# Four heads on 32 partitions each: moving Q and K in 4 KB runs in a cross-covariance attention kernel

## The chip, the cores and the metric

The kernel runs on one core of one Trainium2 chip. Times are microseconds of the device for one whole execution. A profile's span goes from the first to the last instruction on the core and is some 2 us shorter than the time of the same run (138.7 against 140.83 us in the kernel before). The engines are PE (matrix multiply, with PEld for its weight loads), DVE (vector), ACT (scalar), POOL (GpSimd) and SP, which here only issues DMA.

On one core a run is marked slow when it is more than 1.5% above the fastest of the same kernel; comparisons use the fast runs.

## The reference, cut to what matters

```python
# Q, K, V: (8, 12, 512, 64) float32
Q_norm = Q / (norm of Q over the 512 rows + 1e-10)
K_norm = K / (norm of K over the 512 rows + 1e-10)
attn = einsum('bhnd,bhne->bhde', Q_norm, K_norm)      # 64 x 64 for each head
attn = softmax(attn, axis=-1)
return einsum('bhnd,bhde->bhne', V, attn)
```

There are 96 heads. Q, K, V and the output are 12.58 MB each, 50.3 MB in all, and the arithmetic is small, so a kernel that hides its compute is limited by the transfers (in the kernel before they are 76% of the chain that ended last).

## The kernel before

A unit is 4 heads, and 24 units go through a software pipeline. The norms and the products are had from one matrix: with x = [Q K] for one head (512 rows, 128 columns, bf16), the **gram** xᵀx holds QᵀQ, QᵀK and KᵀK. The diagonal gives the squared norms, and a corner gives the unscaled logits.

Q and K are loaded with 4 consecutive rows of one head on a partition, which is 4 x 64 x 4 B = 1 KB in one piece:

```python
Qf = Q.rearrange("b h (p t) d -> p (b h) t d", p=128)      # t = 4
Kf = K.rearrange("b h (p t) d -> p (b h) t d", p=128)
```

One gram is then 4 matmuls of 128 rows, 16 for a unit. The gram pool has two buffers, so two units' grams lie in different buffers of PSUM:

```python
ps_g = ctx.enter_context(tc.tile_pool(name="ps_g", bufs=2, space=bass.MemoryType.PSUM))
...
def grams(u):
    g = gram[u] = ps_g.tile([128, PU, 4, D], F32, name="gram")
    for h in range(HU):
        o = g[:, h // 2, 2 * (h % 2):2 * (h % 2) + 2, :]
        for t in range(T):
            x = qkb[u][:, h, t, :]
            nc.tensor.matmul(o, x, x, start=(t == 0), stop=(t == T - 1))
```

The order in which one pipeline step `s` issues its work is the order of each engine's queue:

```python
on(casts, s + CAST_AHEAD)   # DVE  f32 -> bf16 of Q and K
on(scale_k, s - 1)          # DVE  reads the gram, writes kqs
on(normalise, s - 2)        # DVE
on(grams, s)                # PE
on(norms, s)                # DVE  reads the gram; then POOL: power -1/2, gives rq
on(cast_v, s - 1)           # DVE
on(vtrans, s - 2)           # PE, then ACT
on(outs, s - 3)             # PE, then ACT
on(logits, s - 1)           # PE   kqs times an identity
on(doubled, s - 2)          # PE, then ACT
on(exps, s - 1)             # ACT
```

Of the kernel before, what the change touches and what calls it, by code (L numbers as in the profile page):

```python
# [8 lines left out]
F32 = mybir.dt.float32  # L9
BF16 = mybir.dt.bfloat16  # L10
AF = mybir.ActivationFunctionType
ALU = mybir.AluOpType

D = 64
T = 4
HU = 4
PU = HU // 2
RV = 16
NV = 512 // RV
HS = 128 // NV  # L20
SV = HU // HS
TP = RV // 2


@with_exitstack
def kernel(
# [9 lines left out]
    assert N == 128 * T and Q.shape[3] == D  # L36
    BH = B * H
    U = BH // HU



    Qf = Q.rearrange("b h (p t) d -> p (b h) t d", p=128)
    Kf = K.rearrange("b h (p t) d -> p (b h) t d", p=128)
    Vf = V.rearrange("b h n d -> (b h n d)").rearrange("(s p f) -> p s f", p=128, f=RV * D)
    Of = out.rearrange("b h n d -> (b h n d)").rearrange("(s p f) -> p s f", p=128, f=RV * D)
# [11 lines left out]
    ps_g = ctx.enter_context(tc.tile_pool(name="ps_g", bufs=2, space=bass.MemoryType.PSUM))  # L57
    ps_v = ctx.enter_context(tc.tile_pool(name="ps_v", bufs=2, space=bass.MemoryType.PSUM))
    ps_l = ctx.enter_context(tc.tile_pool(name="ps_l", bufs=1, space=bass.MemoryType.PSUM))
    ps_d = ctx.enter_context(tc.tile_pool(name="ps_d", bufs=1, space=bass.MemoryType.PSUM))  # L60
# [7 lines left out]
    qf, kf, vf, vb, qkb, gram, nsq, kqs, rq, lg, ex, at, ab, vt, so = ({} for _ in range(15))  # L68

    def load_qk(u):  # L70
        qf[u] = qp.tile([128, HU, T, D], F32, name="qf")
        kf[u] = qp.tile([128, HU, T, D], F32, name="kf")
        nc.sync.dma_start(out=qf[u], in_=Qf[:, u * HU:(u + 1) * HU])  # L73
        nc.sync.dma_start(out=kf[u], in_=Kf[:, u * HU:(u + 1) * HU])  # L74

    def load_v(u):
        vf[u] = vp.tile([128, SV, RV * D], F32, name="vf")
        nc.sync.dma_start(out=vf[u], in_=Vf[:, u * SV:(u + 1) * SV])  # L78

    def store(u):  # L80
        nc.sync.dma_start(out=Of[:, u * SV:(u + 1) * SV], in_=so[u])

    def casts(u):

        t_ = qkb[u] = qkp.tile([128, HU, T, 2 * D], BF16, name="qkb")
        nc.vector.tensor_copy(t_[:, 0::2, :, 0:D], qf[u][:, 0::2])  # L86
        nc.vector.tensor_copy(t_[:, 1::2, :, D:2 * D], qf[u][:, 1::2])
        nc.vector.tensor_copy(t_[:, 0::2, :, D:2 * D], kf[u][:, 0::2])  # L88
        nc.vector.tensor_copy(t_[:, 1::2, :, 0:D], kf[u][:, 1::2])  # L89

    def cast_v(u):
        w = vb[u] = vbp.tile([128, SV, TP, 2 * D], BF16, name="vb")
        nc.vector.tensor_copy(w.rearrange("p s t d -> p s (t d)"), vf[u])  # L93

    def grams(u):
        g = gram[u] = ps_g.tile([128, PU, 4, D], F32, name="gram")
        for h in range(HU):
            o = g[:, h // 2, 2 * (h % 2):2 * (h % 2) + 2, :]
            for t in range(T):
                x = qkb[u][:, h, t, :]  # L100
                nc.tensor.matmul(o, x, x, start=(t == 0), stop=(t == T - 1))  # L101

    def norms(u):

        n2 = nsq[u] = small.tile([128, 2, PU], F32, name="nsq")
        for p in range(PU):
            for c, (blk, m) in enumerate(((gram[u][:, p, 0::3, :], mask_q), (gram[u][:, p, 1:3, :], mask_k))):
                scr = small.tile([128, 2, D], F32, name="scr")
                nc.vector.tensor_tensor_reduce(  # L109
                    out=scr, in0=blk, in1=m, scale=1.0, scalar=1e-20,  # L110
                    op0=ALU.mult, op1=ALU.add, accum_out=n2[:, c, p:p + 1],
                )
        r = rq[u] = small.tile([128, 2, PU], F32, name="rq")
        nc.gpsimd.tensor_tensor(out=r, in0=n2, in1=mhalf, op=ALU.pow)  # L114

    def scale_k(u):

        kk = kqs[u] = small.tile([128, PU, 2, D], F32, name="kqs")
        for p in range(PU):
            nc.vector.scalar_tensor_tensor(  # L120
                out=kk[:, p], in0=gram[u][:, p, 0::3, :], scalar=rq[u][:, 1, p:p + 1], in1=off_diag,
                op0=ALU.mult, op1=ALU.mult,
            )

    def logits(u):
        l = lg[u] = ps_l.tile([128, PU, D], F32, name="lg")
        for p in range(PU):
            nc.tensor.matmul(l[:, p, :], kqs[u][:, p].rearrange("p a d -> p (a d)"), eye2)  # L128

    def exps(u):  # L130
        e = ex[u] = small.tile([128, PU, D], F32, name="ex")
        s = small.tile([128, PU], F32, name="esum")
        for p in range(PU):
            nc.scalar.activation(e[:, p, :], lg[u][:, p, :], AF.Exp, scale=rq[u][:, 0, p:p + 1], accum_out=s[:, p:p + 1])  # L134
        ex[u] = (e, s)

    def normalise(u):
        e, s = ex[u]
        ri = small.tile([128, PU], F32, name="rinv")
        nc.vector.reciprocal(ri, s)  # L140
        a = at[u] = small.tile([128, PU, D], BF16, name="at")
        for p in range(PU):
            nc.vector.tensor_scalar_mul(a[:, p, :], e[:, p, :], ri[:, p:p + 1])  # L143
# [120 lines left out]
```

## Time and profile before

| | before |
|---|---|
| time, median of 3 (range) | 141.01 us (140.42 to 141.5) |
| span and mean granted PE clock of the profiled run | 138.7 us, 0.842 |
| DMA: packets, mean rate | 32,274, 365 GB/s |
| chain that ended last | 76% DMA |

The lines that carry the reading are in the prediction below. Two more of the page are needed later, the busy time of each engine (us, share of the span, instructions) and the one POOL operation (busy time and mean ns of one, then POOL's idle time and what ended it):

```profile
PE 90.0 (65%) x1488; PEld 77.3 (56%) x1488; DVE 95.7 (69%) x432; ACT 82.9 (60%) x217; POOL 38.3 (28%) x45
...
L114 POOL TENSOR_TENSOR rq<-nsq,mhalf 128x4 f32<-128x4 f32 x24 | 34.1, 1419 | 87.8 <-DVE nsq L109 74.0
```

No engine is above 70%. PE has 1,488 matmuls and as many weight loads. Nothing but the DMA is near its limit: its engines are 90% busy or more from the second of the 40 slices to the 37th.

### The profile page before, as it was taken

How to read it: one execution, taken by the hardware profiler on the slowest of the kernel's cores; microseconds unless marked ns; L12 is line 12 of the kernel's file. 1: busy time of each engine (PE TensorE's matmuls, PEld its weight loads, DVE VectorE, ACT ScalarE, POOL GpSimd, SP SyncE). 2: the span in 40 equal slices, each digit the busy share in tenths (PEclk: the TensorE clock that was granted, in tenths of full speed). 3: DMA queues.
4: the chain of work that ended last, by engine and by line, in shares of the span. 5: the costliest groups of instructions: out<-in, count | busy, mean ns of one | idle time of the engine just before them, and what ended most of it. 6: DMA issues, size and time to landing. Idle time of an engine off the chain costs nothing.

```text
span 138.7 us, 4018 instructions
## 1 busy us (share of the span) xinstructions
PE 90.0 (65%) x1488; PEld 77.3 (56%) x1488; DVE 95.7 (69%) x432; ACT 82.9 (60%) x217; POOL 38.3 (28%) x45
## 2 busy tenths in 40 slices
PE   0135779686765766776677667568398757686830
PEld 0124779565554655655665656566398647565720
DVE  0626978989895876876966967866868868877200
ACT  0000356978778458557567567477367585588970
POOL 7403304432133214214224134033043141133000
PEclk9999999999999879779779779779655896896555
DMA  4999999999999999999999999999999999999643
GB/s 129 321 344 374 369 368 362 365 371 367 365 366 387 398 389 393 394 393 393 393 398 391 394 400 389 395 392 390 398 398 385 395 399 389 412 418 395 281 177 151
DMA packets 32274, 50.58 MB, mean 365 GB/s; under 512 B 1536, under 2 KB 26112, under 8 KB 32256
## 3 DMA queue, kind: packets, MB, share of 16 engines
q1 hardware_dynamic: 32256, 50.34, 99.3%
q8 instruction: 11, 0.18, 0.5%
q14 instruction: 7, 0.06, 0.1%
HBM read 37.75 MB, written 12.58 MB: 363 GB/s over the span
## 4 chain that ended last, share of the span: by engine, by line
DMA 76%; DVE 8%; SPq 5%; ACT 3%; PE 3%; issue 1%; POOL 1%; ACTq 0%; POOLq 0%
DMA kf<-in_K_dram 76%; SPq L73 2%; DVE scr L109 2%; SPq L74 2%; DVE qkb L88 2%; DVE kqs L120 2%; DVE at L143 1%; PE po L171 1%; ACT so L175 1%; SPq L78 1%; POOL rq L114 1%; PE lg L128 1%; PE vps L159 1%; DVE qkb L89 1%; ACT vt L161 1%
## 5 line engine op out<-in xcount | busy, mean ns | idle before, releaser
L114 POOL TENSOR_TENSOR rq<-nsq,mhalf 128x4 f32<-128x4 f32 x24 | 34.1, 1419 | 87.8 <-DVE nsq L109 74.0
L101 PE MATMUL gram<-qkb 128*128 128x128 bf16 x384 | 35.0, 263 | 9.4 <-DVE qkb L88 9.4
L101 PEld LDWEIGHTS <-qkb 128*128 128x128 bf16 x384 | 31.4, 122 | 9.7 <-DVE qkb L88 9.7
L128 PE MATMUL lg<-eye,kqs 128*128 128x64 f32 x96 | 18.3, 323 | 28.0 <-DVE kqs L120 24.0
L128 PEld LDWEIGHTS lg<-eye,kqs 128*128 128x128 f32 x96 | 15.3, 227 | 32.0 <-ACT so L175 18.6
L161 ACT COPY vt<-vps 128x1024 bf16<-128x1024 bf16 x24 | 24.3, 1012 | 13.4 <-PE vps L159 13.4
L175 ACT COPY so<-po 128x512 f32<-128x512 f32 x48 | 26.0, 599 | 0.7 <-PE po L171 0.7
L159 PE MATMUL vps<-identb,vb 128*128 128x128 bf16 x192 | 20.0, 265 | 4.4 <-DVE vb L93 4.4
L86 DVE CAST qkb<-qf 128x512 bf16<-128x512 f32 x24 | 10.8, 451 | 16.8 <-DMA qf<-in_Q_dram 16.7
L151 ACT CAST ab<-dup 64x256 bf16<-64x256 f32 x24 | 8.8, 367 | 20.9 <-PE dup L149 20.9
L88 DVE CAST qkb<-kf 128x512 bf16<-128x512 f32 x24 | 10.2, 427 | 14.1 <-DMA kf<-in_K_dram 14.0
L159 PEld LDWEIGHTS <-vb 128*128 128x128 bf16 x192 | 15.8, 123 | 6.7 <-DVE vb L93 6.6
L171 PE MATMUL po<-ab,vt 128*32 128x128 bf16 x768 | 18.0, 247 | 1.5 <-ACT ab L152 1.5
L93 DVE CAST vb<-vf 128x1024 bf16<-128x1024 f32 x24 | 16.5, 689 | 0.0
L171 PEld LDWEIGHTS <-vt 128*32 128x32 bf16 x768 | 13.5, 110 | 5.0 <-issue 3.4
L120 DVE SCALAR_TENSOR_TENSOR kqs<-gram,rq,off_diag 128x128 f32<-128x128 f32 x48 | 14.5, 344 | 1.8 <-POOL rq L114 1.8
L134 ACT ACTIVATE ex<-lg,rq 128x64 f32<-128x64 f32 x48 | 14.6, 309 | 0.6
L109 DVE CUSTOM_DVE_ANT_0 scr<-gram,swap 128x128 f32<-128x128 f32 x48 | 13.7, 286 | 0.0
L109 DVE CUSTOM_DVE_ANT_0 scr<-gram,ident 128x128 f32<-128x128 f32 x48 | 13.7, 286 | 0.0
L134 ACT ACT_TABLE_LOAD x1 | 1.3, 1283 | 16.1 <-PE lg L128 16.1
L143 DVE TENSOR_SCALAR at<-ex,rinv 128x64 bf16<-128x64 f32 x48 | 10.0, 252 | 0.9
L89 DVE CAST qkb<-kf 128x512 bf16<-128x512 f32 x24 | 10.1, 420 | 0.0
(23 smaller groups left out, 56.8 us busy)
## 6 DMA issues: line engine op xcount, KB each, us to landing
qf<-in_Q_dram SPq DMA_DIRECT2D x24, 512.0 KB, 9.5
kf<-in_K_dram SPq DMA_DIRECT2D x24, 512.0 KB, 10.4
vf<-in_V_dram SPq DMA_DIRECT2D x24, 512.0 KB, 10.3
out_dram<-so SPq DMA_DIRECT2D x24, 512.0 KB, 9.2
```

Of the source, the lines that this page charges most:

```text
L88: nc.vector.tensor_copy(t_[:, 0::2, :, D:2 * D], kf[u][:, 0::2])
L93: nc.vector.tensor_copy(w.rearrange("p s t d -> p s (t d)"), vf[u])
L101: nc.tensor.matmul(o, x, x, start=(t == 0), stop=(t == T - 1))
L109: nc.vector.tensor_tensor_reduce(out=scr, in0=blk, in1=m, scale=1.0, scalar=1e-20, op0=ALU.mult, op1=ALU.add, accum_out=n2[:, c, p:p + 1],)
L114: nc.gpsimd.tensor_tensor(out=r, in0=n2, in1=mhalf, op=ALU.pow)
L120: nc.vector.scalar_tensor_tensor(out=kk[:, p], in0=gram[u][:, p, 0::3, :], scalar=rq[u][:, 1, p:p + 1], in1=off_diag, op0=ALU.mult, op1=AL ...
L128: nc.tensor.matmul(l[:, p, :], kqs[u][:, p].rearrange("p a d -> p (a d)"), eye2)
L134: nc.scalar.activation(e[:, p, :], lg[u][:, p, :], AF.Exp, scale=rq[u][:, 0, p:p + 1], accum_out=s[:, p:p + 1])
L159: nc.tensor.transpose(ps[:, g, t, :], vb[u][:, g, t, :], identb)
L161: nc.scalar.copy(w, ps)
L171: nc.tensor.matmul(po[NV * x:NV * (x + 1), k, :], vt[u][:, g, t, NV * x:NV * (x + 1)], ab[u][:, h // 2, h % 2].rearrange("p a d -> p (a d) ...
L175: nc.scalar.copy(s.rearrange("p g t d -> p (g t) d")[:, 4 * i:4 * i + 4, :], po)
```

## The change

The intent is to have every transfer in runs of 4 KB. A unit's 4 heads are flattened, so a partition gets 16 consecutive rows of one head and each head has 32 partitions. All else follows from that layout: a gram is 16 matmuls of 32 rows, and the four heads use the four row groups of the PE array side by side, each with its own slice of one PSUM tile; the logits are unpadded, and the softmax of 4 heads is one pass. The diff, cut to its core:

```diff
-    Qf = Q.rearrange("b h (p t) d -> p (b h) t d", p=128)
-    Kf = K.rearrange("b h (p t) d -> p (b h) t d", p=128)
...
+    Qf, Kf, Vf, Of = (x.rearrange("b h n d -> (b h n d)").rearrange("(u p f) -> u p f", p=128, f=R * D) for x in (Q, K, V, out))
...
-    ps_g = ctx.enter_context(tc.tile_pool(name="ps_g", bufs=2, space=bass.MemoryType.PSUM))
+    ps_g = ctx.enter_context(tc.tile_pool(name="ps_g", bufs=1, space=bass.MemoryType.PSUM))
...
+    gbuf = ps_g.tile([128, HU, 4, 2 * D], F32, name="gram")     # one tile, a slice for each head
...
     def grams(u):
+        g = gbuf[:, :, u % 2]        # units alternate between columns of the same tile
+        for t in range(R):
+            for h in range(HU):
+                x = qkb[u][NV * h:NV * (h + 1), t, :]
+                nc.tensor.matmul(g[:, h], x, x, start=(t == 0), stop=(t == R - 1), tile_position=(NV * h, 0))
...
     def scale_k(u):
+        kk = kqs[u] = small.tile([128, HU, D], F32, name="kqs")
+        nc.vector.tensor_tensor(
+            out=kk[D:], in0=gbuf[D:, :, u % 2, 0:D], in1=rq[u][D:, :, None].to_broadcast([D, HU, D]), op=ALU.mult,
+        )
...
+    def scale_q(u):
+        s = sl[u] = small.tile([D, HU, D], F32, name="sl")
+        nc.vector.tensor_tensor(out=s, in0=lg, in1=rq[u][0:D, :, None].to_broadcast([D, HU, D]), op=ALU.mult)
...
         on(grams, s)
         on(norms, s)
-        on(cast_v, s - 1)
         on(vtrans, s - 2)
         on(outs, s - 3)
         on(logits, s - 1)
+        on(scale_q, s - 1)
+        on(cast_v, s - 1)
```

( Left out: the casts, now two of 1024 elements; exp, sum, reciprocal and multiply on 64x256; the constants no longer needed. Two PSUM pools also shrink: the V transposes have one buffer in place of two, and the logits and the duplicate of the softmax share one tile.)

More of the change, by code (lines that the diff above doesn't have):

```diff
@@ L12 @@
 ALU = mybir.AluOpType
+AX = mybir.AxisListType
 D = 64
-T = 4
 HU = 4
-PU = HU // 2
-RV = 16
-NV = 512 // RV
-HS = 128 // NV
-SV = HU // HS
-TP = RV // 2
+NV = 32
+R = 16
+TP = R // 2
 @with_exitstack
@@ L35 @@
     B, H, N, _ = Q.shape
-    assert N == 128 * T and Q.shape[3] == D
-    BH = B * H
-    U = BH // HU
-    Qf = Q.rearrange("b h (p t) d -> p (b h) t d", p=128)
-    Kf = K.rearrange("b h (p t) d -> p (b h) t d", p=128)
-    Vf = V.rearrange("b h n d -> (b h n d)").rearrange("(s p f) -> p s f", p=128, f=RV * D)
-    Of = out.rearrange("b h n d -> (b h n d)").rearrange("(s p f) -> p s f", p=128, f=RV * D)
+    assert N == NV * R and Q.shape[3] == D
+    U = B * H // HU
+    Qf, Kf, Vf, Of = (x.rearrange("b h n d -> (b h n d)").rearrange("(u p f) -> u p f", p=128, f=R * D) for x in (Q, K, V, out))
     ctx.enter_context(tc.manual_schedule())
@@ L56 @@
     small = ctx.enter_context(tc.tile_pool(name="small", bufs=4))
-    ps_g = ctx.enter_context(tc.tile_pool(name="ps_g", bufs=2, space=bass.MemoryType.PSUM))
-    ps_v = ctx.enter_context(tc.tile_pool(name="ps_v", bufs=2, space=bass.MemoryType.PSUM))
+    ps_g = ctx.enter_context(tc.tile_pool(name="ps_g", bufs=1, space=bass.MemoryType.PSUM))
+    ps_v = ctx.enter_context(tc.tile_pool(name="ps_v", bufs=1, space=bass.MemoryType.PSUM))
     ps_l = ctx.enter_context(tc.tile_pool(name="ps_l", bufs=1, space=bass.MemoryType.PSUM))
-    ps_d = ctx.enter_context(tc.tile_pool(name="ps_d", bufs=1, space=bass.MemoryType.PSUM))
     ps_o = ctx.enter_context(tc.tile_pool(name="ps_o", bufs=2, space=bass.MemoryType.PSUM))
@@ L66 @@
     STORE_LAG = 6
-    qf, kf, vf, vb, qkb, gram, nsq, kqs, rq, lg, ex, at, ab, vt, so = ({} for _ in range(15))
+    qf, kf, vf, vb, qkb, nsq, rq, kqs, sl, ex, vt, so = ({} for _ in range(12))
     def load_qk(u):
-        qf[u] = qp.tile([128, HU, T, D], F32, name="qf")
-        kf[u] = qp.tile([128, HU, T, D], F32, name="kf")
-        nc.sync.dma_start(out=qf[u], in_=Qf[:, u * HU:(u + 1) * HU])
-        nc.sync.dma_start(out=kf[u], in_=Kf[:, u * HU:(u + 1) * HU])
+        qf[u] = qp.tile([128, R, D], F32, name="qf")
+        kf[u] = qp.tile([128, R, D], F32, name="kf")
+        nc.sync.dma_start(out=qf[u].rearrange("p t d -> p (t d)"), in_=Qf[u])
+        nc.sync.dma_start(out=kf[u].rearrange("p t d -> p (t d)"), in_=Kf[u])
@@ L76, in load_v @@
     def load_v(u):
-        vf[u] = vp.tile([128, SV, RV * D], F32, name="vf")
-        nc.sync.dma_start(out=vf[u], in_=Vf[:, u * SV:(u + 1) * SV])
+        vf[u] = vp.tile([128, R * D], F32, name="vf")
+        nc.sync.dma_start(out=vf[u], in_=Vf[u])
     def store(u):
-        nc.sync.dma_start(out=Of[:, u * SV:(u + 1) * SV], in_=so[u])
+        nc.sync.dma_start(out=Of[u], in_=so[u].rearrange("p t d -> p (t d)"))
     def casts(u):
-        t_ = qkb[u] = qkp.tile([128, HU, T, 2 * D], BF16, name="qkb")
@@ L86, in casts @@
-        nc.vector.tensor_copy(t_[:, 0::2, :, 0:D], qf[u][:, 0::2])
-        nc.vector.tensor_copy(t_[:, 1::2, :, D:2 * D], qf[u][:, 1::2])
-        nc.vector.tensor_copy(t_[:, 0::2, :, D:2 * D], kf[u][:, 0::2])
-        nc.vector.tensor_copy(t_[:, 1::2, :, 0:D], kf[u][:, 1::2])
+        t_ = qkb[u] = qkp.tile([128, R, 2 * D], BF16, name="qkb")
+        nc.vector.tensor_copy(t_[:, :, 0:D], qf[u])
+        nc.vector.tensor_copy(t_[:, :, D:], kf[u])
     def cast_v(u):
-        w = vb[u] = vbp.tile([128, SV, TP, 2 * D], BF16, name="vb")
@@ L93, in cast_v @@
-        nc.vector.tensor_copy(w.rearrange("p s t d -> p s (t d)"), vf[u])
+        w = vb[u] = vbp.tile([128, TP, 2 * D], BF16, name="vb")
+        nc.vector.tensor_copy(w.rearrange("p t d -> p (t d)"), vf[u])
     def grams(u):
-        g = gram[u] = ps_g.tile([128, PU, 4, D], F32, name="gram")
-        for h in range(HU):
-            o = g[:, h // 2, 2 * (h % 2):2 * (h % 2) + 2, :]
-            for t in range(T):
-                x = qkb[u][:, h, t, :]
-                nc.tensor.matmul(o, x, x, start=(t == 0), stop=(t == T - 1))
@@ L103, in norms @@
-    def norms(u):
-        n2 = nsq[u] = small.tile([128, 2, PU], F32, name="nsq")
-        for p in range(PU):
-            for c, (blk, m) in enumerate(((gram[u][:, p, 0::3, :], mask_q), (gram[u][:, p, 1:3, :], mask_k))):
-                scr = small.tile([128, 2, D], F32, name="scr")
-                nc.vector.tensor_tensor_reduce(
-                    out=scr, in0=blk, in1=m, scale=1.0, scalar=1e-20,
-                    op0=ALU.mult, op1=ALU.add, accum_out=n2[:, c, p:p + 1],
-                )
-        r = rq[u] = small.tile([128, 2, PU], F32, name="rq")
+        g = gbuf[:, :, u % 2]
@@ new lines, in grams, with norms @@
+        for t in range(R):
+            for h in range(HU):
+                x = qkb[u][NV * h:NV * (h + 1), t, :]
+                nc.tensor.matmul(g[:, h], x, x, start=(t == 0), stop=(t == R - 1), tile_position=(NV * h, 0))
+    def norms(u):
+        n2 = nsq[u] = small.tile([128, HU], F32, name="nsq")
+        for h in range(HU):
+            scr = small.tile([128, 2 * D], F32, name="scr")
+            nc.vector.tensor_tensor_reduce(
+                out=scr, in0=gbuf[:, h, u % 2], in1=ident, scale=1.0, scalar=1e-20,
+                op0=ALU.mult, op1=ALU.add, accum_out=n2[:, h:h + 1],
+            )
+        r = rq[u] = small.tile([128, HU], F32, name="rq")
@@ L114, in norms @@
         nc.gpsimd.tensor_tensor(out=r, in0=n2, in1=mhalf, op=ALU.pow)
     def scale_k(u):
-        kk = kqs[u] = small.tile([128, PU, 2, D], F32, name="kqs")
-        for p in range(PU):
-            nc.vector.scalar_tensor_tensor(
-                out=kk[:, p], in0=gram[u][:, p, 0::3, :], scalar=rq[u][:, 1, p:p + 1], in1=off_diag,
-                op0=ALU.mult, op1=ALU.mult,
-            )
-    def logits(u):
-        l = lg[u] = ps_l.tile([128, PU, D], F32, name="lg")
-        for p in range(PU):
-            nc.tensor.matmul(l[:, p, :], kqs[u][:, p].rearrange("p a d -> p (a d)"), eye2)
@@ L130, in exps @@
-    def exps(u):
-        e = ex[u] = small.tile([128, PU, D], F32, name="ex")
-        s = small.tile([128, PU], F32, name="esum")
-        for p in range(PU):
-            nc.scalar.activation(e[:, p, :], lg[u][:, p, :], AF.Exp, scale=rq[u][:, 0, p:p + 1], accum_out=s[:, p:p + 1])
-        ex[u] = (e, s)
+        kk = kqs[u] = small.tile([128, HU, D], F32, name="kqs")
+        nc.vector.tensor_tensor(
+            out=kk[D:], in0=gbuf[D:, :, u % 2, 0:D], in1=rq[u][D:, :, None].to_broadcast([D, HU, D]), op=ALU.mult,
+        )
@@ L137, in normalise @@
+    def logits(u):
+        for h in range(HU):
+            nc.tensor.matmul(lg[:, h, :], kqs[u][D:, h, :], ident[D:, D:], tile_position=(D, 0))
+    def scale_q(u):
+        s = sl[u] = small.tile([D, HU, D], F32, name="sl")
+        nc.vector.tensor_tensor(out=s, in0=lg, in1=rq[u][0:D, :, None].to_broadcast([D, HU, D]), op=ALU.mult)
+    def exps(u):
+        e = ex[u] = small.tile([D, HU, D], F32, name="ex")
+        nc.scalar.activation(e, sl[u], AF.Exp)
     def normalise(u):
-        e, s = ex[u]
@@ L139, in normalise @@
-        ri = small.tile([128, PU], F32, name="rinv")
+        s = small.tile([D, HU], F32, name="esum")
+        nc.vector.reduce_sum(out=s, in_=ex[u], axis=AX.X)
+        ri = small.tile([D, HU], F32, name="rinv")
         nc.vector.reciprocal(ri, s)
-        a = at[u] = small.tile([128, PU, D], BF16, name="at")
-        for p in range(PU):
-            nc.vector.tensor_scalar_mul(a[:, p, :], e[:, p, :], ri[:, p:p + 1])
+        a = abuf[u % len(abuf)]
+        nc.vector.tensor_tensor(out=a[0:D, :, 0, :], in0=ex[u], in1=ri[:, :, None].to_broadcast([D, HU, D]), op=ALU.mult)
@@ L145, in doubled @@
     def doubled(u):
-        d = ps_d.tile([128, 2, PU, D], F32, name="dup")
-        for c in range(2):
-            nc.tensor.matmul(d[:, c], pick[:, c, :], at[u])
-        a = ab[u] = abuf[u % len(abuf)]
-        nc.scalar.copy(a[0:D, :, :, 0, :], d[0:D].rearrange("p c u d -> p u c d"))
-        nc.scalar.copy(a[D:, :, :, 1, :], d[D:].rearrange("p c u d -> p u c d"))
-    def vtrans(u):
-        ps = ps_v.tile([128, SV, TP, 128], BF16, name="vps")
-        for g in range(SV):
-            for t in range(TP):
-                nc.tensor.transpose(ps[:, g, t, :], vb[u][:, g, t, :], identb)
-        w = vt[u] = vtp.tile([128, SV, TP, 128], BF16, name="vt")
+        a = abuf[u % len(abuf)]
@@ L161, in vtrans @@
+        nc.tensor.matmul(dup[D:], identb[0:D, 0:D], a[0:D, :, 0, :], tile_position=(0, D))
+        nc.scalar.copy(a[D:, :, 1, :], dup[D:])
+    def vtrans(u):
+        ps = ps_v.tile([128, TP, 128], BF16, name="vps")
+        for t in range(TP):
+            nc.tensor.transpose(ps[:, t, :], vb[u][:, t, :], identb)
+        w = vt[u] = vtp.tile([128, TP, 128], BF16, name="vt")
         nc.scalar.copy(w, ps)
     def outs(u):
-        s = so[u] = sop.tile([128, SV, TP, 2 * D], F32, name="so")
+        s = so[u] = sop.tile([128, TP, 2 * D], F32, name="so")
+        a = abuf[u % len(abuf)]
@@ L165, in outs @@
         for i in range(2):
-            po = ps_o.tile([128, 4, 2 * D], F32, name="po")
-            for k in range(4):
-                g, t = divmod(4 * i + k, TP)
-                for x in range(HS):
-                    h = g * HS + x
+            po = ps_o.tile([128, TP // 2, 2 * D], F32, name="po")
+            for k in range(TP // 2):
+                for h in range(HU):
+                    rows = slice(NV * h, NV * (h + 1))
                     nc.tensor.matmul(
-                        po[NV * x:NV * (x + 1), k, :], vt[u][:, g, t, NV * x:NV * (x + 1)],
-                        ab[u][:, h // 2, h % 2].rearrange("p a d -> p (a d)"), tile_position=(0, NV * x),
-                    )
@@ L175, in outs @@
-            nc.scalar.copy(s.rearrange("p g t d -> p (g t) d")[:, 4 * i:4 * i + 4, :], po)
+                        po[rows, k, :], vt[u][:, TP // 2 * i + k, rows],
+                        a[:, h].rearrange("p a d -> p (a d)"), tile_position=(0, NV * h),
+                    )
+            nc.scalar.copy(s[:, TP // 2 * i:TP // 2 * (i + 1), :], po)
+    gbuf = ps_g.tile([128, HU, 4, 2 * D], F32, name="gram")
+    ltile = ps_l.tile([128, 2, HU, D], F32, name="lgdup")
+    lg = ltile[0:D, 0]
+    dup = ltile[:, 1]
@@ L186 @@
     nc.gpsimd.tensor_copy(identb, ident)
-    mask_q = ident.rearrange("p (a d) -> p a d", a=2)
-    swap = const.tile([128, 2, D], F32, name="swap")
-    nc.gpsimd.tensor_copy(swap[:, 0, :], ident[:, D:])
-    nc.gpsimd.tensor_copy(swap[:, 1, :], ident[:, :D])
-    mask_k = swap
-    eye2 = const.tile([128, D], F32, name="eye2")
-    nc.gpsimd.tensor_tensor(out=eye2, in0=ident[:, :D], in1=ident[:, D:], op=ALU.add)
-    off_diag = const.tile([128, 2, D], F32, name="off_diag")
-    nc.gpsimd.memset(off_diag, 0.0)
-    nc.gpsimd.memset(off_diag[0:D, 1, :], 1.0)
-    nc.gpsimd.memset(off_diag[D:, 0, :], 1.0)
-    pick = const.tile([128, 2, 128], BF16, name="pick")
-    for c in range(2):
-        for i in range(2):
-            nc.gpsimd.tensor_copy(pick[:, c, i * D:(i + 1) * D], ident[:, c * D:(c + 1) * D])
+    mhalf = const.tile([128, HU], F32, name="mhalf")
+    nc.gpsimd.memset(mhalf, -0.5)
     abuf = []
     for i in range(3):
-        a = const.tile([128, PU, 2, 2, D], BF16, name=f"ab{i}")
+        a = const.tile([128, HU, 2, D], BF16, name=f"ab{i}")
         nc.gpsimd.memset(a, 0.0)
         abuf.append(a)
-    mhalf = const.tile([128, 2, PU], F32, name="mhalf")
-    nc.gpsimd.memset(mhalf, -0.5)
     for u in range(CAST_AHEAD):
```

## The prediction

Of the softmax's 0.42 + 0.16 + 0.42 the 0.16 is the reciprocal of the kernel before.

> **What bounds the kernel now.** I read the page's slices first, then the chain that ended last, the windows, the groups, and the timeline of single steps.
>
> ```profile
> PEclk9999999999999879779779779779655896896555
> DMA  4999999999999999999999999999999999999643
> GB/s 129 321 344 374 369 368 362 365 371 367 365 366 387 398 389 393 394 393 393 393 398 391 394 400 389 395 392 390 398 398 385 395 399 389 412 418 395 281 177 151
> ...
> DMA 76%; DVE 8%; SPq 5%; ACT 3%; PE 3%; issue 1%; POOL 1%; ACTq 0%; POOLq 0%
> ```
>
> The DMA engines are 90% busy or more from the second slice to slice 37, and 76% of the chain is the K load. So bytes per second set the time. The rate has three levels: about 367 GB/s while only Q, K and V are loaded, about 394 once stores join, 410 to 420 at the end. The end is the telling stretch: K has landed for the last time at 119.3 us, and only V and stores, both in 4 KB runs, are left.
>
> ```profile
> 28.00:32.00 4.00, 2.75 (x62) 2.16 (x61) 3.63 (x17) 3.21 (x10) 1.30 (x1) 1.00 1.08 367
> 56.00:60.00 4.00, 3.52 (x42) 3.22 (x46) 3.22 (x17) 1.54 (x7) 1.58 (x1) 0.68 1.06 397
> 122.00:124.00 2.00, 1.58 (x48) 1.16 (x45) 1.10 (x4) 1.68 (x6) 1.30 (x1) 1.00 1.03 420
> ```
>
> (Windows: stretch, length, busy time of PE, weight load, DVE, ACT, POOL, then clock, DMA share, GB/s.) A unit of 4 heads moves 4 x 524,288 B = 2.097 MB; at 396 GB/s that is 5.30 us, and two K loads in a row on the chain are 10.58 us apart (65.98, 76.57): two units. Beneath that, one step of compute reads so:
>
> ```profile
> 65.83 0.43 DVE L88 CAST qkb<-kf 128x512 bf16<-128x512 f32 x1 [0.62 <-DMA kf<-in_K_dram]
> 66.17 0.42 DVE L89 CAST qkb<-kf 128x512 bf16<-128x512 f32 x1
> 66.51 0.60 DVE L120 SCALAR_TENSOR_TENSOR kqs<-gram,rq,off_diag 128x128 f32<-128x128 f32 x2
> ...
> 67.55 0.28 DVE L109 CUSTOM_DVE_ANT_0 scr<-gram,ident 128x128 f32<-128x128 f32 x1
> ...
> 67.88 1.91 PE L101 MATMUL gram<-qkb 128*128 128x128 bf16 x16
> ...
> 73.13 1.06 PE L101 MATMUL gram<-qkb 128*128 128x128 bf16 x16
> 73.70 0.69 DVE L93 CAST vb<-vf 128x1024 bf16<-128x1024 f32 x1
> 74.45 0.62 PE L159 MATMUL vps<-identb,vb 128*128 128x128 bf16 x8 [0.27 <-DVE vb L93]
> 75.00 0.63 PE L171 MATMUL po<-ab,vt 128*32 128x128 bf16 x32
> ...
> 77.59 0.79 PE L128 MATMUL lg<-eye,kqs 128*128 128x64 f32 x4 [1.96 <-DVE kqs L120]
> ```
>
> Two things matter. The gram of the next unit (67.88) runs on PE at the same time as DVE reads the present gram (67.55 on): [...]PE is always one unit ahead and DVE waits for DMA alone. And PE has two speeds that alternate here from step to step: 1.06 against 1.91 us for the same 16 matmuls. DVE's step, from start to start, is casts 4 x 0.34 = 1.36, scale_k 0.52, reciprocal and normalise 0.52, norms 4 x 0.21 = 0.84, V cast 0.69: 3.93 us, 94 us in 24 units (the page has 95.7). It has 1.3 us a unit to spare.
>
> [...]L171, which packs four column tiles, does 32 matmuls in 0.63 us. [...]the SBUF casts show 0.52 ns an element (0.69 less 0.42 over 512)[...].
>
> **The change part by part.**
> DMA: Q and K packets fall from 24,576 of 1 KB to 6,144 of 4 KB. At 416 GB/s (mean of 410, 420, 418) a unit takes 5.04 us, 0.26 less. On its own over 24 units that is about 6 us.
>
> DVE per unit (estimates): two casts of 1024 instead of four of 512, 1.30 (each like the V cast, 0.69, overlapping a little); norms 0.84 as before; scale_k one op of 64x256 out of PSUM, 0.344 or 0.286 (the two 128-element ops)[...], say 0.45; scale_q, new, 0.45; softmax sum, new, reciprocal and one multiply, 0.42 + 0.16 + 0.42 = 1.00; V cast 0.65. Sum 4.69 against 3.93: DVE goes to about 113 us. Still under 5.04, but the slack is gone.
>
> ACT: four exps with accumulator reads become one exp, two duplicate copies become one: down some 0.7 us, off the path.
>
> PE: grams become 64 matmuls of 32 rows. With four row groups overlapping they are 16 rounds, like the 16 full ones: 1.06 us plus issue, and 64 at the packed rate of L171 are 1.26; I take 1.25 fast, 2.0 slow. Logits 4 smaller fp32 products, 0.65 (0.9). Transposes and outputs stay: 0.55 and 0.55 from start to start, 0.95 and 1.0 slow.
>
> The part that decides is none of these sums but the **gram's PSUM**. All four heads' grams of a unit now lie in four banks, and the next unit's grams in other columns of the *same* four banks. [...]the gram of unit s must then wait until scale_k of unit s-1 has read, and scale_k stands on DVE behind the casts of s+1. PE's run-ahead is lost. Transposes, outputs and logits stand behind the gram in PE's order; scale_q waits for the logits; the V cast stands behind scale_q; the next casts behind that. It closes into one loop, in us at fast clock (slow):
> casts 1.30 + scale_k 0.45 + hand-over 0.1 + gram 1.25 (2.0) + transposes 0.55 (0.95) + outputs 0.55 (1.0) + logits 0.65 (0.9) + hand-over 0.1 + scale_q 0.45 + V cast 0.65 = 6.05 (7.90).
> Norms and normalise fit in the wait. The hand-over is that from kqs to lg: first scale_k starts 66.51, takes some 0.34, logits' weights load at 66.97. 6.05 is more than DMA's 5.04 and than today's 5.3, in every step.
>
> The whole: casts of unit 0 can be done near 6.6 us as now, the second K lands near 8, the three filling steps cost about 13, so step 3 starts near 21. Then 20 full steps, one without casts (P - 1.3), and the drain: last scale_k to last output 7.5, store and end 3.5 (the shortest landing was 2.6). Span = 21 + 20P + P - 1.3 + 11 = 30.7 + 21P; a run is 2.3 us longer than the span (141.0 against 138.7). All fast: 160. All slow: 199. PE will idle 2 to 3 us in each step, and the present steps, with gaps of that kind, alternate. With about a quarter to a third slow, P is some 6.45: 168.
>
> **The rivals.**
> (a) *The loop does not close*, because [...]the hand-overs fall early. Then DMA bounds at 5.04 a unit once stores run; the load-only stage (7 units at 4.24 now, of 1.57 MB) gains nothing, for DVE needs 4.69. Total about 141 - 16 x 0.26 - 1 for a quicker start, some 135, up to 137. For it: the author moved the V cast behind scale_q, a place that only makes sense if scale_q does not wait.[...]
> (b) *Row groups do not overlap*: 64 x 0.066 (1.06/16) = 4.2 us per gram. P is 9.0 and the run over 215. For it: every matmul brings new weights[...]. Against: L171 packs with new weights each time.
> (c) *The loop closes but PE stays fast*, or small ops cost less than I took: P near 5.6, about 150.
>
> **Range and chances.** [...]I give it 0.78, with (c) within. Rival (a) has about 0.16, and 0.06 is for a loop that ends just at today's 5.3 (P under 5.3 gives 144). (b) has some 0.05 within slower. The range of 144 to 190 holds the loop at any mix of clocks but the slowest, and leaves (a) and (b) out.
>
> **What would show it.** Right: the gram on PE starts just after scale_k and waits for it by name, also where DMA is idle; scale_q waits for the logits 0.5 to 2 us a step; DMA share falls to some 80% and below, GB/s to 300 to 340; the chain changes from DMA to DVE and PE in turn; DVE busy is near 113 us and one gram 1.2 to 2.0. Wrong: grams that start while DVE still reads the gram before, DMA share staying at 9 with about 415 GB/s; or single grams of 4 us. It would also be wrong if scale_q and scale_k took 0.3 rather than 0.45 and PE stayed at full clock.

## The result, and the profile after

| | before | after |
|---|---|---|
| time, median of 4 (range) | 141.25 us (140.42 to 142.27) | 179.45 us (178.63 to 181.21) |
| span, PE clock (profiled run) | 138.7 us, 0.842 | 177.2 us, 0.804 |
| DMA packets, mean rate | 32,274, 365 GB/s | 13,850, 286 GB/s |
| chain that ended last | DMA 76% | PE 51%, DVE 32% |

The change is **slower**: the ratio is 1.272 (95% interval 1.259 to 1.285). Here and below, a ratio is the mean time of one kernel's fast runs over that of the kernel before in the same rounds, so it is not quite the ratio of the medians quoted. Results are correct.

From the page of the kernel after: busy times, then the slices (tenths of full clock, tenths of DMA time, GB/s) and the chain by engine.

```profile
PE 104.3 (59%) x2712; PEld 84.9 (48%) x2712; DVE 110.2 (62%) x384; ACT 68.0 (38%) x121; POOL 29.0 (16%) x35
...
PEclk9999999686786786876876876867867867869995
DMA  5999999999999889898898898898865273033244
GB/s 215 382 421 411 410 403 409 411 409 413 378 378 340 258 352 312 276 363 285 279 362 268 287 388 252 295 355 265 322 230 142 102 235 122 0 122 122 118 184 175
...
PE 51%; DVE 32%; DMA 4%; issue 3%; ACT 3%; POOL 2%; SPq 1%; ACTq 0%; POOLq 0%
```

After the start and up to a quarter of the span the loads run at 400 to 421 GB/s, better than the 367 of before, so the 4 KB runs do what they were meant to. Then the rate falls to some 250 to 390. That is where compute falls behind and gives its buffers back late (the issues of the V loads wait 68.3 us in all for the V cast). No engine is busier than 62%, and the DMA is not the limit either, so what is left is a loop of waits. The windows view of 20 us in the middle (the columns are those of the prediction's windows) has PE busy for 13.0 of 20 us at a granted clock of 0.74, and 313 GB/s:

```profile
80.00:100.00 20.00, 12.98 (x339) 10.53 (x339) 13.24 (x48) 7.90 (x14) 3.02 (x3) 0.74 0.90 313
```

The chain in order of time (start, us, what) shows the loop itself. Read it as a relay in which each line starts when the one above is done:

```profile
94.19 0.44 DVE kqs L105
94.63 0.04 issue
94.67 1.89 PE gram L88 x57
96.56 0.97 PE vps L139 x8
97.53 0.59 PE po L151 x20
98.12 0.62 PE lgdup L111 x8
98.74 0.02 issue
98.76 0.42 DVE sl L115
99.18 0.60 DVE vb L80
99.78 0.60 DVE qkb L75
100.38 0.60 DVE qkb L76
100.98 0.03 issue
101.01 0.44 DVE kqs L105
```

It comes back to scale_k (`kqs`) after 101.01 - 94.19 = 6.82 us: scale_k, gram, V transposes, outputs, logits, scale_q (`sl`), V cast, the two casts of Q and K, scale_k. DVE and PE take turns and neither works ahead. The waits of the same step, on the timeline (the bracket holds the idle time before and what ended it) and in the table of waits (us in total, times, longest):

```profile
94.67 1.89 PE L88 MATMUL gram<-qkb 32*128 32x128 bf16 x64 [2.00 <-DVE kqs L105]
...
161.74 1.07 PE L88 MATMUL gram<-qkb 32*128 32x128 bf16 x64 [0.79 <-DVE kqs L105]
```

```profile
PE gram L88 <- DVE kqs L105: 47.9, 23, 4.6
DVE sl L115 <- PE lgdup L111: 27.8, 22, 1.8
```

The gram of one unit waits in 23 of 24 units for the scale_k of the unit before. That read concerns *other columns*, but the same tile, `gbuf`. The last gram, at full clock, takes 1.07 us for 64 matmuls of 32 rows, each with its own weight load; the 16 matmuls of 128 rows took 1.06 before. The row groups do run side by side, and the gram itself costs no more than it did.

### The profile page after: what moved, and what is told of

Its sections match the earlier page's. It is cut to its first block, busy times and chain, and to the rows that moved or that the text cites. A ratio compares the mean times of both kernels' runs of the same rounds, so it can differ in the third digit from the quotient of the medians.

```text
span 177.2 us, 6265 instructions
## 1 busy us (share of the span) xinstructions
PE 104.3 (59%) x2712; PEld 84.9 (48%) x2712; DVE 110.2 (62%) x384; ACT 68.0 (38%) x121; POOL 29.0 (16%) x35
## 2 busy tenths in 40 slices
DMA packets 13850, 50.72 MB, mean 286 GB/s; under 512 B 1536, under 2 KB 1536, under 8 KB 13824
## 4 chain that ended last, share of the span: by engine, by line
PE 51%; DVE 32%; DMA 4%; issue 3%; ACT 3%; POOL 2%; SPq 1%; ACTq 0%; POOLq 0%
PE gram L88 24%; PE vps L139 12%; PE lgdup L111 8%; PE po L151 8%; DVE vb L80 7%; DVE qkb L76 7%; DVE qkb L75 7%; DVE kqs L105 6%; DVE sl L115 5%; DMA kf<-in_K_dram 4%; POOL rq L100 2%; ACT so L155 2%; DVE scr L95 1%; ACT ab L133 1%; ACT ex L119 0%
## 5 line engine op out<-in xcount | busy, mean ns | idle before, releaser
L88 PE MATMUL gram<-qkb 32*128 32x128 bf16 x1536 | 44.4, 302 | 54.0 <-DVE kqs L105 47.9
L88 PEld LDWEIGHTS <-qkb 32*128 32x128 bf16 x1536 | 40.1, 137 | 69.4 <-issue 61.2
L115 DVE TENSOR_TENSOR sl<-lgdup,rq 64x256 f32<-64x256 f32 x24 | 10.0, 417 | 28.0 <-PE lgdup L111 27.8
L75 DVE CAST qkb<-qf 128x1024 bf16<-128x1024 f32 x24 | 16.3, 680 | 5.5 <-DMA qf<-in_Q_dram 5.5
L111 PE MATMUL lgdup<-ident,kqs 64*64 64x64 f32 x192 | 17.4, 235 | 0.0
L76 DVE CAST qkb<-kf 128x1024 bf16<-128x1024 f32 x24 | 16.3, 680 | 1.5 <-DMA kf<-in_K_dram 1.5
L80 DVE CAST vb<-vf 128x1024 bf16<-128x1024 f32 x24 | 16.2, 675 | 0.0
L119 ACT ACTIVATE ex<-sl 64x256 f32<-64x256 f32 x24 | 10.0, 417 | 14.5 <-DVE sl L115 14.0
L111 PEld LDWEIGHTS lgdup<-ident,kqs 64*64 64x64 f32 x192 | 14.0, 144 | 2.9 <-issue 0.8
L132 PE MATMUL lgdup<-ab,identb 64*64 64x256 bf16 x24 | 6.6, 275 | 12.3 <-DVE sl L115 11.7
L105 DVE TENSOR_TENSOR kqs<-gram,rq 64x256 f32<-64x256 f32 x24 | 10.3, 428 | 0.9
L127 DVE TENSOR_TENSOR ab<-ex,rinv 64x256 bf16<-64x256 f32 x24 | 10.0, 417 | 0.8
```

Of the source, the lines that this page charges most:

```text
L75: nc.vector.tensor_copy(t_[:, :, 0:D], qf[u])
L76: nc.vector.tensor_copy(t_[:, :, D:], kf[u])
L80: nc.vector.tensor_copy(w.rearrange("p t d -> p (t d)"), vf[u])
L88: nc.tensor.matmul(g[:, h], x, x, start=(t == 0), stop=(t == R - 1), tile_position=(NV * h, 0))
L105: nc.vector.tensor_tensor(out=kk[D:], in0=gbuf[D:, :, u % 2, 0:D], in1=rq[u][D:, :, None].to_broadcast([D, HU, D]), op=ALU.mult,)
L111: nc.tensor.matmul(lg[:, h, :], kqs[u][D:, h, :], ident[D:, D:], tile_position=(D, 0))
```

## The experiments

**Theory (T):** the PSUM tile that two units' grams share forces gram(s) behind scale_k(s-1), and program order closes the loop shown above. **Rivals:** the small matmuls themselves are slow (R1), the packets or the transfers cost time (R2), or the new DVE work is too much (R3). One rival has no run: two units in different places of PSUM but in *one* tile. So the runs can show that scale_k's read of the gram's tile holds the next gram back, and not whether the order goes by the place or by the tile. Twelve kernels were run; before took 141.2 to 141.7 us beside all of them. "Wrong" means that the outputs are wrong by design and the times still count.

### Is it the transfers? Two runs

**The kernel before, with Q and K in 4 KB runs, nothing else** (wrong: rows of different heads meet in a gram):

```diff
-        nc.sync.dma_start(out=qf[u], in_=Qf[:, u * HU:(u + 1) * HU])
+        nc.sync.dma_start(out=qf[u].rearrange("p h t d -> p (h t d)"), in_=Qf[u])   # K alike
```

> The kernel before with one edit: Q and K are loaded as 4 KB runs into the same tiles. The result is wrong on purpose, every operation and size stays. It measures the DMA part of the change by itself. Theory (bytes per second bound that kernel): steady GB/s from 394 to 410 to 418, a unit from 5.30 to 5.07, 133 to 137 us. Rival (packet size does not matter at these rates): 141.

Measured: 133.04 us (132.56 to 133.16), ratio 0.941 (0.935 to 0.946). The transfer part alone is worth 8 us.

**The kernel after, with Q and K in 1 KB runs again** (wrong):

```diff
-        nc.sync.dma_start(out=qf[u].rearrange("p t d -> p (t d)"), in_=Qf[u])
+        nc.sync.dma_start(out=qf[u].rearrange("p (h t) d -> p h t d", h=HU), in_=Qf[:, u * HU:(u + 1) * HU])   # K alike
```

> The changed kernel with Q and K loaded in 1 KB runs as before into the same tiles; the result is wrong on purpose. Theory (DMA does not bound the changed kernel, a step is 6.83 us where the transfers of a unit need 5.3 even with 1 KB runs): 177 to 182 us, the load-only start a little later. Rival (the 4 KB runs still earn something): 5 us or more slower than 179.5.

Measured: 180.76 us (178.99 to 181.45), against 179.45 with 4 KB. The same step that is worth 8 us in the kernel before is worth 1 us or nothing in the kernel after. R2 falls, and the gain is not lost to a flaw in the transfers: it is hidden behind the loop.

### Is it the shared gram tile? Two runs

**scale_k reads a constant in SBUF in place of the gram** (wrong; same instruction, same size):

```diff
-            out=kk[D:], in0=gbuf[D:, :, u % 2, 0:D], in1=rq[u][D:, :, None].to_broadcast([D, HU, D]), op=ALU.mult,
+            out=kk[D:], in0=fake[D:], in1=rq[u][D:, :, None].to_broadcast([D, HU, D]), op=ALU.mult,
```

> The changed kernel in which scale_k reads a constant of the same shape in SBUF instead of the gram in PSUM; the result is wrong on purpose, the order of all instructions stays. Bank theory: only scale_k's read[...] holds the gram back; without it the gram runs right after the step before, during the casts, and scale_q finds its logits ready: DVE or DMA bounds near 5.1 a unit, 133 to 141 us. Rival (PE's order or its clock makes the loop[...]): within 3% of 179.

Measured: 145.62 us (145.2 to 146.97). 34 us go with one operand, while all 64 small matmuls, all DVE work and all transfers stay. So R1 and R3 can't be the main cause. It ends 4 to 5 us over the expected range, though.

**ACT copies the K rows of the gram to SBUF early, and scale_k reads the copy** (correct results):

```diff
+        c = kraw[u] = small.tile([128, HU, D], F32, name="kraw")
+        nc.scalar.copy(c[D:], gbuf[D:, :, u % 2, 0:D])              # right after the norms
...
-            out=kk[D:], in0=gbuf[D:, :, u % 2, 0:D], in1=rq[u][D:, :, None].to_broadcast([D, HU, D]), op=ALU.mult,
+            out=kk[D:], in0=kraw[u][D:], in1=rq[u][D:, :, None].to_broadcast([D, HU, D]), op=ALU.mult,
```

> The changed kernel in its own order, with ACT copying the K rows of the gram to SBUF right after the norms, and scale_k reading the copy; correct result.[...] Bank theory: as with the constant, the gram runs a unit ahead again; what then bounds is norms 0.85 + power 2.9 (beside the casts) + scale_k 0.44 + normalise 1.0 with hand-overs, 5.3 to 5.5 a step: 142 to 150 us. Rival (only the constant's missing data dependence made that run fast): 165 or more.

Measured: 148.19 us (147.52 to 148.67), ratio 1.051 (1.043 to 1.058). A correct kernel with one instruction *more* for each unit wins 31 of the 38 us back, because the last read of the gram's tile now falls right after the norms. What bounds it now? Its chain in order of time:

```profile
82.63 2.81 POOL rq L102
85.47 0.42 DVE kqs L107
...
87.97 2.88 POOL rq L102
```

A second loop, of 87.97 - 82.63 = 5.34 us: power on POOL, scale_k, normalise, the next norms, power. More than half of it is one POOL operation on 128x4 elements.

### The second loop: POOL beside DVE casts. Two runs

**Transposes and outputs ahead of the gram in PE's order** (correct):

```diff
-        on(grams, s)
-        on(norms, s)
         on(vtrans, s - 2)
         on(outs, s - 3)
+        on(grams, s)
+        on(norms, s)
         on(logits, s - 1)
```

> The changed kernel with one edit: in PE's order the transposes and outputs of the older units stand before the gram of this unit. Correct result. Loop theory (gram waits for scale_k[...], and transposes 0.96, outputs 0.59 stand between gram and logits): these two leave the loop and fill the time in which PE now waits, PE stays warm, the gram falls from 1.9 to 1.07 us; the loop is casts 1.2 + scale_k 0.44 + gram 1.07 + logits 0.62 + scale_q 0.42 + V cast 0.60 + hand-overs 0.1 = 4.5, so DVE (4.6) or DMA (5.1 a unit) bounds: 133 to 139 us. Rival (PE's or DVE's work itself, not its order, sets 6.83 a step): within 3% of 179.

Measured: 171.01 us (168.15 to 172.16), a clear miss. Two of its four runs count as slow, so no ratio was formed; the two fast ones took 168.15 and 169.97. The gram's wait did shrink from 2.0 to 0.5 us. But two things took its place. PE ran at half clock for much of the time (0.50 from 60 to 80 us, 0.67 from 80 to 100, mean 0.665), and scale_k now waits for POOL:

```profile
96.42 3.04 POOL L100 TENSOR_TENSOR rq<-nsq,mhalf 128x4 f32<-128x4 f32 x1 [3.54 <-DVE nsq L95]
96.72 0.68 DVE L80 CAST vb<-vf 128x1024 bf16<-128x1024 f32 x1
...
97.32 0.68 DVE L75 CAST qkb<-qf 128x1024 bf16<-128x1024 f32 x1
...
97.92 0.68 DVE L76 CAST qkb<-kf 128x1024 bf16<-128x1024 f32 x1
...
99.50 0.43 DVE L105 TENSOR_TENSOR kqs<-gram,rq 64x256 f32<-64x256 f32 x1 [0.90 <-POOL rq L100]
```

The same operation takes 1.01 us in the middle of the kernel after, where DVE does no cast beside it:

```profile
97.69 1.01 POOL L100 TENSOR_TENSOR rq<-nsq,mhalf 128x4 f32<-128x4 f32 x1 [5.82 <-DVE nsq L95]
```

In the step of this run DVE runs its three casts from 96.72 to 98.60: 1.88 us, and 1.01 + 1.88 = 2.89 is nearly the whole of the 3.04. In the copy-out run the casts fill 83.51 to 85.39, again 1.88 us, and the power takes 2.81. In both traces POOL's operation is longer by about the casts' whole time (2.03 and 1.80 us more than 1.01), though by the profile, whose spans on POOL are rough, it had begun 0.30 and 0.88 us before the first cast. Why the casts hold it up is not shown. Before, it took 1.42 us on average (the L114 line) and 1.07 to 1.59 in single units, so it may have been stretched there too at times, but little hung on it (scale_k waited 1.8 us for it in all).

**The same order, with the power replaced by a reciprocal on DVE** (wrong, for it lacks the root):

```diff
-        nc.gpsimd.tensor_tensor(out=r, in0=n2, in1=mhalf, op=ALU.pow)
+        nc.vector.reciprocal(r, n2)
```

> The run with transposes first once more, but the power of -0.5 on GpSimd (2.9 to 3.0 us there) is replaced by a reciprocal on DVE; wrong result on purpose. In that run each step took 6.57 us as gram 1.9 + norms 0.85 + power 3.04 + scale_k 0.44 with their hand-overs. Theory (that second loop[...] took over): without it the first loop is left, at half clock casts 1.2 + scale_k 0.44 + gram 1.9 + logits 1.1 + scale_q 0.42 + V cast 0.6 = 5.7, at full clock 4.5 and so DMA's 5.1: 135 to 152 us. Rival (the cold PE sets the step, not GpSimd): within 3% of 171.

Measured: 157.03 us (155.04 to 158.36, one of four runs slow), 14 us below the run above, or 13 by the means of the fast runs. POOL's share of the second loop is shown. What remains are steps of 5.70 us on average (15 of them from 42.09 to 127.58 us), many of them partly at half clock (mean 0.743). The expected 5.7 is their mean, but the first loop alone does not set it: the chain goes by turns through the casts and scale_k and through norms, V cast, transposes and outputs.

### PE's clock: two runs

**V cast back in its old place, right after the norms** (correct). It takes 0.60 us out of the loop:

```diff
         on(norms, s)
+        on(cast_v, s - 1)
         on(vtrans, s - 2)
         on(outs, s - 3)
         on(logits, s - 1)
         on(scale_q, s - 1)
-        on(cast_v, s - 1)
```

> The changed kernel with the V cast put back where it stood before the change, right after the norms and so before scale_q on DVE. Correct result. Loop theory: the V cast, 0.60, leaves the loop and falls into DVE's wait for the logits: a step goes from 6.83 to some 6.2, 21 steps save 13: 164 to 168 us, less if PE warms. Rival (DVE's sum of work counts, the place doesn't): 179.

Measured: 177.23 us (176.85 to 179.85, one of four runs slow), ratio 1.253 (1.245 to 1.262). The V cast did leave the loop, and its 0.60 us with it. But from 80 to 100 us the granted clock was 0.59 in place of 0.74. In the step at 90.4 us the gram took 1.90, transposes 0.97, outputs 0.97 and logits 0.99, together 4.83 against 4.07 in the step shown above. 0.76 more and 0.60 less: that step is 6.99 us. The expected 164 to 168 was missed; most of the saving on paper went to the clock.

**16 spare matmuls in front of each gram, to fill PE's idle time** (correct; they write to a buffer of the output pool):

```diff
     def grams(u):
+        if u >= 1:
+            wm = ps_o.tile([128, 4, 2 * D], F32, name="po")
+            for i in range(NW):                       # NW = 16
+                nc.tensor.matmul(wm[:, i % 4, :], identb, identb)
```

> The changed kernel with 16 spare matmuls (identity times identity, into an output bank that is written over later) before each gram in PE's order, where PE now waits 2.0 us for scale_k. Correct result. Theory that the wait is what makes PE cold: it stays at full clock, gram 1.9 to 1.07, transposes 0.96 to 0.55; a step goes from 6.83 to 5.6 and the run to 153 to 160 us. Rival (what lowers the clock is something other than the wait, as the 0.665 of the run with transposes first suggests, where PE hardly waited and was slow all the same): clock stays at 0.8 or falls, 179 to 195 us.

Measured: 164.1 us (160.99 to 165.18, two of four runs slow), ratio of the fast ones 1.148 (1.137 to 1.158); the mean clock was 0.947, up from 0.804. More work on PE makes the kernel 15 us faster (18 by the means of the fast runs), so about that much of the 38 hangs on the half clock. (It is not to be added to the 31 to 34 above: without the loop PE does not wait so long. In the run with the constant no gram waits for scale_k.) It is short of the expected 153 to 160. Steps at full clock take 5.6 to 6.2 us, where 5.6 was expected, but between 85 and 107 us steps were at half clock for a part (7.1 us from 92.71 to 99.80), and some outputs have a pause in the middle that the profile puts down to nothing:

```profile
63.95 0.52 PE L156 MATMUL po<-ab,vt 128*32 128x128 bf16 x24 [0.45 <-issue]
```

Such pauses come back below.

### Looking for a better order: four runs

**The gram early in the step, right behind scale_k** (correct; gram(0) is issued before the loop):

```diff
+ casts(s+1), cast_v(s-1), norms(s), vtrans(s-2), outs(s-3), logits(s-1), scale_q(s-1),
+ exps(s-1), normalise(s-2), doubled(s-2), scale_k(s), grams(s+1)
```

> The changed kernel, same instructions, new order; correct result. DVE: casts, V cast, norms, scale_q, normalise, scale_k of the same unit; PE: transposes, outputs, logits, duplicate, then the gram of the next unit. The gram then waits for a scale_k that is followed by casts and V cast, so it runs beside these, and the power runs beside scale_q and normalise, where it should take 1.0 to 1.4 us and not 3. Theory: no loop left above DMA's 5.1 a unit unless PE is cold throughout (5.3): 133 to 143 us, at best 5% under the kernel before. Rival (four row groups cost PE too much in any order): over 150.

Measured: 180.79 us (179.5 to 181.48), ratio 1.278. A miss, and mine: the logits stand on PE behind gram, transposes and outputs; scale_q on DVE waits for them (the profile names ACT's copy of the outputs, which ends within 0.1 us of the logits); and scale_k, which releases the next gram, stands behind scale_q. I had cut one loop and closed another, of 6.9 us at half clock.

**scale_k in front of scale_q, and the power beside the softmax in place of the casts** (correct):

```diff
+ norms(s), vtrans(s-2), outs(s-3), logits(s-1), normalise(s-2), scale_k(s), grams(s+1),
+ scale_q(s-1), exps(s-1), doubled(s-2), cast_v(s-1), casts(s+2)
```

> The changed kernel, same instructions, third order; correct result. The run with the new order closed a loop of its own: scale_q waited for logits that stood behind gram, transposes and outputs on PE, and scale_k behind scale_q. Here DVE does norms, normalise (during which the power runs), scale_k, scale_q, V cast, casts; PE does transposes, outputs, logits, then the next gram, then the duplicate. The gram then overlaps scale_q, V cast and casts (2.2 us), and transposes, outputs and logits overlap norms, normalise and power. Loop at full clock: gram 1.07 + norms 0.85 + power 1.0 to 1.4 + scale_k 0.44 = 3.5 to 3.8; PE alone 3.4 at full and 5.4 at half clock; DVE alone 4.6. Theory: DMA bounds again at 5.1 a unit or PE at 5.4: 133 to 142 us. Rival (something in the changed layout costs time in every order): over 150.

Measured: 146.85 us (144.45 to 147.81, three of six runs slow by the 1.5% rule), ratio of the fast ones 1.033 (1.024 to 1.041). The power took 1.01 us in each of the seven units looked at, so both loops are open. Still it is not at 133. Loads run ahead at some 410 GB/s (415 with the stores from 80 to 100 us), so compute is the limit, and PE is busy for 16.2 of the 20 us from 80 on, at a clock of 0.65. (Its profiled run is one of the slow ones.)

**As above, with the V cast on ACT and moved up** (correct; takes 0.6 us a unit off DVE):

```diff
-        nc.vector.tensor_copy(w.rearrange("p t d -> p (t d)"), vf[u])
+        nc.scalar.copy(w.rearrange("p t d -> p (t d)"), vf[u])
```

> The run with the power beside the softmax, with one more edit: the V cast runs on ACT, which is 47% busy there, instead of DVE. Correct result. In that run a step took 4.7 us where PE was at full clock (DVE's own sum) and 5.2 where it was not, so compute never got ahead of the transfers as it does in the kernel before. Theory (DVE's sum is now the bound): DVE falls to 4.05 a step, ACT rises to 3.9, PE is 3.4 at full clock; compute can run ahead in the load-only stage and DMA bounds after it: 133 to 141 us. Rival (PE at half clock, 5.3 a step, is the bound): 143 to 149 us, no gain.

Measured: 145.62 us (144.5 to 146.44), ratio 1.033 (1.026 to 1.039). DVE's busy time fell from 106.8 to 93.3 us, and the time didn't move. DVE's sum is not the limit, and the expectation's rival, 143 to 149, came. What the trace does show are holes in PE's work that nothing ends:

```profile
55.94 0.40 PE L151 MATMUL po<-ab,vt 128*32 128x128 bf16 x8 [2.30 <-issue]
```

There PE stops 2.30 us in the middle of one unit's outputs, with its data ready. "Issue" means that the profile sees no cause. There are 11 such holes, 16.3 us in all. I had not expected them, and read the transfer records of this run for a cause. The profile lists packets of instructions among its transfers: 18 in this run from 28 to 130 us (0.29 MB), and in the whole of the kernel after 21 (0.34 MB), which is, if all are PE's, 5,424 / 21 = 258 PE instructions to a packet; the kernel before had 11 for 2,976, or 271. Three things tie the holes to them:

- For each of the 11 holes, an instruction packet starts between 2.75 and 2.2 us before the hole's end. Such packets come about every 6 us, so chance would give one.
- The holes sit at the same places of the program in this run and in the run before it, which has the same PE order: eight of them have the same number of matmuls of their group left.
- Where four holes in a row fall into grams, 50, 35, 20 and 5 matmuls of the gram are left. A unit has 5,424 / 24 = 226 PE instructions, and 15 matmuls with their weight loads are 30: the holes are 226 + 30 = 256 instructions apart, about what comes to one packet.

The run with the spare matmuls is a test that nobody planned. It has 16 matmuls more with their weight loads, so 226 + 32 = 258 PE instructions a unit, and a hole every 256 must come one matmul earlier from unit to unit. In the steps at 45 and 51 us and in that at 63 us, two steps on, the pause stands after 11, 10 and 8 of the outputs.

So I read the holes as PE out of instructions, while the transfers run at 412 to 415 GB/s (60 to 100 us). That is read from the traces; no experiment changed the supply of instructions alone.

**As above, with half of each gram's sum** (wrong: 8 of 16 rows, so 32 matmuls and 32 weight loads fewer a unit):

```diff
-        for t in range(R):
+        for t in range(R // 2):
```

> Wrong on purpose. The kernel with the V cast on ACT took 145.6 us though DMA and DVE were both cut; its PE was 70% busy, half of the steps at half clock, with up to 2.4 us between two matmuls that the profile marks as issue. Here each gram sums 8 of its 16 rows only: 32 small matmuls and 32 weight loads a unit fewer, nothing else changed. Theory (PE, in its clock and its issue of many small matmuls, is what keeps this order above the kernel before): the gram falls by about half, 0.5 us a step at full clock and 0.95 at half clock plus its share of the issue gaps, so 21 steps give back 10 us or more, and the time falls to 134 to 138, where the loads and the stores at the end set it. Rival (order of the stores at the end, DVE or the DMA sets it): within 2 us of 145.6.

Measured: 134.19 us (133.33 to 135.48, one of four runs slow), ratio 0.947 (0.937 to 0.956). The page's chain by engine:

```profile
DMA 59%; DVE 15%; PE 7%; POOL 5%; ACT 5%; issue 4%; SPq 1%; ACTq 0%; POOLq 0%; DVEq 0%
```

Now the DMA bounds, at the time that 4 KB runs allow (133.0 in the kernel before). PE's matmuls show no wait on "issue" at all, with 3,888 instructions in place of 5,424. PE was what kept the reordered kernels at 146, by its holes (16.3 us in the run above, none here) and its time at half clock. This run cuts both at once, so it doesn't tell their shares apart.

No version with correct results beat the kernel before. The best of them, at 145.6, is 3% slower.

## Why the prediction was right

**The bound of the kernel before: right.** With 4 KB runs and nothing else it fell to 133.0. I had put the gain at about 6 us; it was 8. Rival (a)'s 135 to 137 for a kernel with no loop was not reached by any kernel with whole grams: with the loop open they took 145.6 to 148.2, and only half grams took 134.2.

**The gram waits for scale_k's read: right, and shown** from both sides. The wait is there by name, 47.9 us in 23 units, and taking scale_k's read off the gram's tile gave 34 us (wrong results) or 31 us (correct). Whether the place in PSUM is the reason or the one tile was not shown: no run separates the two.

**The loop: right in its links and their order.** The chain has each of the predicted pieces and no other. Term by term:

| term | predicted, fast (slow) | in the step at 94.19 us |
|---|---|---|
| casts | 1.30 | 1.20 |
| scale_k | 0.45 | 0.44 |
| hand-overs, both | 0.2 | 0.09 |
| gram | 1.25 (2.0) | 1.89 |
| transposes | 0.55 (0.95) | 0.97 |
| outputs | 0.55 (1.0) | 0.59 |
| logits | 0.65 (0.9) | 0.62 |
| scale_q | 0.45 | 0.42 |
| V cast | 0.65 | 0.60 |
| sum | 6.05 (7.90) | 6.82 |

**The term that was mis-sized is the clock's share.** I took "about a quarter to a third slow", steps that alternate as before, and put 0.40 us on the step: 6.45. That sum was itself a slip: a quarter to a third of the 1.85 us between fast and slow is 0.46 to 0.62, so 6.51 to 6.67. In fact *every* full step had its gram and transposes at half clock (grams of 1.67 to 1.90 us), and from 60 us on its outputs and logits at full. With the last gram's 1.07 and the transposes' 0.57 at full clock, the surcharge is 0.82 + 0.40 = 1.22 us. Against that, the rest of the loop was 0.45 us shorter than I had it, mostly from the gram (1.07, not 1.25), the casts and the hand-overs. So 6.05 - 0.45 + 1.22 = 6.82. Over the run the mean step was (155.63 - 24.48) / 19 = 6.90 us, from scale_k's first and last full steps. 21 steps at 6.90 in place of 6.45 are 9.5 us. Fill and drain were 177.2 - 21 x 6.90 = 32.3 against 30.7. 9.5 and 1.6 are the 11 us between 168 and 179.

**The small costs held.** DVE was put at about 113 us busy and had 110.2. scale_k and scale_q, estimated at 0.45 each, took 0.43 and 0.42.

**The signs.** The gram's wait by name, scale_q's wait for the logits (27.8 us over 22 units, 1.3 each), the rate (313 GB/s for 300 to 340) and the chain through PE and DVE in turn all came. The DMA share was only half a sign: the transfer queue's share of the span is 77%, but the windows still have 0.90 in the middle. The GB/s, not the share, told that the DMA had room. Rival (b), row groups one after another, is ruled out by the 1.07 us. Rival (c), PE staying fast, didn't come, but it was no idle thought: the spare matmuls took the kernel part of the way there.

**What I did not see.** Had the first loop been avoided, the kernel would not have reached 135 by itself. Behind it lay the second loop through POOL (146 to 148) and PE itself, with its holes and its half clock (146). The prediction had neither, as neither showed in the kernel before or sets the time of the kernel after.

**What stays open.** What sets PE's clock: it was granted 0.5 from 80 to 100 us in the half-gram run, with PE busy for 16.1 of the 20 us (two steps looked at closely, from 84 to 94 us, had no idle time over 1.8 us), and yet 0.74 in the kernel after, busy for 13.0, where idle times of about 2 us went with half clock in part of each step. Why steps settle so that the same half of each is slow is not shown; from 74 to 156 us the grams start 6.82 to 6.84 us apart, after steps of up to 7.45. And the split of the last 11 us between holes and clock was not measured.

## What to carry to other kernels

Two PSUM buffers in columns of one tile worked here as one buffer (47.9 us of waits in 23 units): ask of every second buffer whether PE can really write it while the first is read. Before you change a layout to feed the DMA better, follow the order of the two or three engines once around a step and ask whether each can still be a unit ahead; a loop of waits shows no busy engine, and it hid an 8 us gain behind a 38 us loss. And when you cut a loop, look at what stands right behind it (here an operation on POOL beside DVE casts, then PE's holes and clock), for the gain ends there.
